# The mixing sub-layer of a two-layer trunk: conv's last projection traced before q's second half, the last tap written to SBUF, two attention steps traced between the value blocks

## The chip, the core and the metric

One Trainium2 chip, of which the kernel uses one core. The metric is the time in microseconds (us) of one execution on the device; where it was run several times, the median stands. A lower time is better.

## The reference, cut to what matters

The input is x of 512 tokens x 1024 features in float32. Two layers follow each other; each is half a SwiGLU network, a mixing sub-layer, and half a SwiGLU network again. The change touches only the mixing sub-layer:

```python
a, g, q, k, v = jnp.split(h @ w_in[l], splits, axis=-1)      # h = rms_norm(x, mix_norm[l]); 512 columns each
conv_out = conv_module(a, g, conv_w[l], conv_b[l], conv_norm[l])
q = rms_norm(q, q_norm[l]); k = rms_norm(k, k_norm[l])       # per head and map, 64 features each
diff_out = diff_attention(q, k, v, rel_bias, lam, lam_init, subln_norm[l])
x = x + jnp.concatenate([conv_out, diff_out], axis=-1) @ w_out[l]

def conv_module(a, g, conv_w, conv_b, conv_norm):
    u = a * jax.nn.sigmoid(g)
    y = causal_depthwise_conv(u, conv_w, width=31) + conv_b    # 512 channels
    return jax.nn.silu(rms_norm(y, conv_norm))                 # norm over the channels

# diff_attention, 4 heads, causal, swept over 4 blocks of 128 queries:
s = jnp.einsum("bhmqd,bhmkd->bhmqk", qi, k) * scale + bias     # m: two maps per head
p = jax.nn.softmax(s, axis=-1)
a = p[:, :, 0] - lam * p[:, :, 1]
o = jnp.einsum("bhqk,bhkd->bhqd", a, v)                        # then rms_norm per head, times (1 - lam_init)
```

`causal_depthwise_conv` stands for the call of `lax.conv_general_dilated` with 30 zeros of padding on the left.

## The kernel before, in words

**Precision.** Products of the projections and of the networks are made in three matmuls: weights and activations are each split into a rounded high part (`whi`, `acth`) and the rest (`wlo`, `actl`), and high x high, high x low and low x high are added up in PSUM. A weight chunk (`chunk`, L103) is loaded by a DMA on SP's queue into `wraw`, ACT copies it to `whi` (L100), and DVE or POOL subtracts to make `wlo` (L101). These three live in rings of 5, 4 and 4 buffers (`RING`, L90): a fifth chunk can only be converted when the chunk that used the slot first has been read by its last matmul. Scores, attention values and transposes are plain float32.

**PSUM.** The eight banks have tags (`BANKS`, L84): two each of `mm`, `sc` and `po`, one `tp`, one `y`. A projection takes a pair of banks, by turn `sc`, `po`, `mm` (`turn_tag`, L320; `pair_banks`, L323), in the order in which the code asks for them.

**Order.** The kernel is traced in a tile framework whose scheduler (`TileContext(..., schedule_with_timeline_sim=True)`, L931) sets the order of the instructions on each engine: it lists them with a modelled timeline, takes what is ready, and breaks ties by the order in which they were traced. A few instructions are pinned by `tc.keep_in_program_order`. So the order of the lines in `mixer` is a priority; it is not yet the order on the engines. Each engine then runs its own list in order and waits on semaphores.

**The mixing sub-layer** (`mixer`, L545) runs from about 355 to 540 us in the first layer and from 1246 to 1430 us in the second. Its steps, with the lines of the kernel before:

- `conv_in(c)` (L552), c = 0 to 3: two weight chunks, two projections of 24 matmuls each (gate and value of 128 conv channels), then the gate: DVE scales the gate by the rows' norm (L572), ACT takes tanh, DVE makes the value, POOL clears 30 columns, DVE writes `u`. c = 0 and 1 are multiplied together (`first_products`, L302).
- `project(which, pair)` (L589): k (which = 1) or q (which = 0), two token blocks (j) of 128 at a time. The four weight chunks of q or k are made at the first pair and kept for the second. 48 matmuls (L600 to L602) go into a pair of banks; ACT squares each block (L608), DVE sums the squares over 64 features (L609), POOL takes the power of -1/2 (`rsqrt`, L223), and DVE writes the normalised block `qn` (L615).
- `to_features(which, pair)` (L635): four transposes per block (L639) into the bank that the projection has left, then ACT copies them out to `kt` (L643) or, twice, to `qz`.
- `project_values(j)` (L621): 24 matmuls for one token block of v, and an ACT copy with the rows' norm.
- `conv_taps(c, n)` (L661): the 31 taps for conv channels c. The first n taps are made by ACT (a product, L671) and POOL (the sum), the others by DVE in a bank of PSUM (L676 or L679, then L684). `POOL_TAPS` = (31, 0, 0, 10): c = 0 is all ACT's and POOL's, c = 1 and 2 are all DVE's, and c = 3 is shared. The result goes to `ys[c]`: for c = 3 a sum of both parts on DVE (L688), for c = 1 and 2 an ACT copy out of PSUM (L690). `conv_square` (L653) squares it on ACT, POOL adds up `csum`.
- `conv_finish` (L693): the norm over channels (`rows_rstd` and `spread`, two passes of transposes), swish (L701 is its scale's product on DVE after ACT's tanh, L703 the low part).
- attention: 16 steps, block i = 3 to 0 and head h = 0 to 3. `attend(n)` (L782) traces the first part of step n and later parts of earlier steps, as a pipeline: `softmaxes` (L709) for step n: two score matmuls (L718), for both maps a DVE instruction that adds the bias and finds the row's minimum (L722) and an ACT exponential with a row sum (L726), then DVE's reciprocal (L729), a factor, and the difference of both maps; `keys_first` (L735) for step n-2: transposes of the map (L739) and an ACT copy (L741); `values` (L744) for step n-3: value matmuls (L748), and after the fourth head the norm per head, written by DVE as `ov` (L763); `block_out` (L771): four transposes and the split into `acth` and `actl`.
- the output projection (L819 to L834): in three rounds, first the conv half of the concatenated features for all tokens, then the attention half for tokens 256 to 511, then for tokens 0 to 255; 12 matmuls each go to a bank `sc` or `po` (`ps_out`), and DVE adds them to x.

**The order in which the body of `mixer` traces them** (L792 to L815): conv_in 0, 1, 2; both halves of k; q's first half with k's transposes around it; q's second half; q's first transposes; conv_in 3; q's last transposes; two attention steps, each with two value blocks behind it; the taps of c = 0 to 3; the attention steps from the third on; conv_finish; the output projection.

The only hand-written order is this one; the body of `mixer`, `conv_taps` and the functions that they call follow, with the lines of the profile.

Of the kernel before, what the change touches and what calls it, by code (L numbers as in the profile page):

```python
# [14 lines left out]
AF = mybir.ActivationFunctionType  # L15
ALU = mybir.AluOpType
# [4 lines left out]
SEQ = 512  # L21
DM = 1024
KT = DM // P
NT = SEQ // P
# [4 lines left out]
CT = CC // P  # L29
TAPS = 31  # L30
PAD = TAPS - 1
# [36 lines left out]
def trunk(ctx: ExitStack, tc: tile.TileContext, xt, par, lamv, relb, onehot,  # L68
          gu1, dn1, wag, wqkv, wout, gu2, dn2, out):
    nc = tc.nc  # L70
    V, S, G, T = nc.vector, nc.scalar, nc.gpsimd, nc.tensor
# [31 lines left out]
    def chunk(src, eng=None):  # L103
        raw, hi, lo = ring("wraw"), ring("whi"), ring("wlo")
        nc.sync.dma_start(raw, src)
        parts_of(raw, hi, lo, eng)
        return hi, lo
# [75 lines left out]
    pars = []  # L183
# [361 lines left out]
    def mixer(l, pr, after):  # L545
        with tc.tile_pool(name="mix", bufs=1) as mp, tc.tile_pool(name="mt", bufs=2) as mt:
            us = [None] * CT
# [4 lines left out]
            def conv_in(c):  # L552

                w = [chunk(wag[l, c, i], V if c < 3 else G) for i in range(2)]
                held.append((c, w, pair_banks(next(turn))))
                if c == 0:
                    return
                if c == 1:
                    row["c"], v, row["b"] = first_products(
                        pr, [h[1] for h in held], [h[2] for h in held], early=True  # L560
                    )

                    row["eps"] = small.tile([P, NT], F32, tag="rowe", name="rowe")
                    V.tensor_scalar(row["eps"], v, HD * EPS, None, op0=ALU.mult)

                    S.activation(small.tile([P, NT], F32, tag="rowx", name="rowx"), row["eps"], AF.Exp)
                else:
                    for i in range(2):
                        products(pr, w, held[-1][2][i], i)
                for n, _, ps in held:  # L570
                    gl = mt.tile([P, SEQ], F32, tag="gl", name="gl", bufs=1)
                    V.tensor_tensor(gl, ps[1], row["b"], op=ALU.mult)  # L572
                    S.activation(gl, gl, AF.Tanh, scale=0.5)
                    al = ps[0]
                    V.scalar_tensor_tensor(al, gl, 1.0, al, op0=ALU.add, op1=ALU.mult)
                    u = mp.tile([P, PAD + SEQ], F32, tag="u", name="u", bufs=4)
                    G.memset(u[:, :PAD], 0.0)
                    V.tensor_tensor(u[:, PAD:], al, row["b"], op=ALU.mult)
                    us[n] = u
                held.clear()  # L580
# [8 lines left out]
            def project(which, pair):  # L589
                if pair == 0:  # L590
                    wts[which] = [chunk(wqkv[l, which, kc], G) for kc in range(KT // 2)]
                w = wts[which]
                js = (2 * pair, 2 * pair + 1)
                ps = pair_banks(next(turn))
                for k in range(KT):
                    wh, wl = wpart(w[k // 2], k % 2, 512)
                    xh, xl = pr[k]
                    for n, j in enumerate(js):
                        t = slice(j * P, (j + 1) * P)
                        T.matmul(ps[n], xh[:, t], wh, start=k == 0, stop=False)  # L600
                        T.matmul(ps[n], xh[:, t], wl, start=False, stop=False)  # L601
                        T.matmul(ps[n], xl[:, t], wh, start=False, stop=k == KT - 1)  # L602

                ep = row["eps"][:, js[0] : js[1] + 1].unsqueeze(2).broadcast_to([P, 2, 8])
                ss = bank("tp", "ps_ss")[:, :16].rearrange("p (j g) -> p j g", j=2)
                for n, j in enumerate(js):
                    sq = tmp.tile([P, SEQ], F32, tag="sq", name="sq")
                    S.activation(sq, ps[n], AF.Square)  # L608
                    V.tensor_reduce(ss[:, n, :], sq.rearrange("p (g d) -> p g d", d=HD), axis=AX.X, op=ALU.add)  # L609
                v = small.tile([P, 2, 8], F32, tag="qkv", name="qkv", bufs=2)  # L610
                V.tensor_tensor(v, ss, ep, op=ALU.add)
                rq = rsqrt(v.rearrange("p j g -> p (j g)"), 16).rearrange("p (j g) -> p j g", j=2)
                for n, j in enumerate(js):
                    qn = mt.tile([P, SEQ], F32, tag="e0", name="qn", bufs=4)
                    V.tensor_tensor(  # L615
                        qn.rearrange("p (g d) -> p g d", d=HD), ps[n].rearrange("p (g d) -> p g d", d=HD),
                        rq[:, n, :].unsqueeze(2).broadcast_to([P, 8, HD]), op=ALU.mult,
                    )
                    qns[which, j] = qn, ps[n]
# [15 lines left out]
            def to_features(which, pair):  # L635
                for j in (2 * pair, 2 * pair + 1):
                    qn, pt = qns[which, j]
                    for h in range(HEADS):
                        T.transpose(pt[:, h * P : (h + 1) * P], qn[:, h * P : (h + 1) * P], ident)  # L639
                    pt = pt.rearrange("p (h t) -> p h t", h=HEADS)  # L640
                    t = slice(j * P, (j + 1) * P)
                    if which == 1:
                        S.activation(kt[:, :, t], pt, AF.Copy)  # L643
                    else:
                        for m in range(2):
                            S.activation(qz[:, m, :, t], pt, AF.Copy, scale=gq[l][:, m : m + 1])
# [3 lines left out]
            ys = [None] * CT  # L650
# [10 lines left out]
            def conv_taps(c, n):  # L661

                wc = _AT["conv_w"] + c * TAPS
                yp = None
                if n:
                    yp = mp.tile([P, SEQ], F32, tag="yp%d" % (n < TAPS), name="yp")
                    G.tensor_scalar(yp, us[c][:, 0:SEQ], pars[l][:, wc : wc + 1], col(l, "conv_b", c),
                                    op0=ALU.mult, op1=ALU.add)
                    for t in range(1, n):
                        p = mt.tile([P, SEQ], F32, tag="prod", name="prod")  # L670
                        S.activation(p, us[c][:, t : t + SEQ], AF.Copy, scale=pars[l][:, wc + t : wc + t + 1])  # L671
                        G.tensor_tensor(yp, yp, p, op=ALU.add)
                if n == TAPS:
                    ys[c] = yp
                    conv_square(c, yp)
                    return  # L676
                y = bank("y", "ps_y")
                if not n:
                    V.tensor_scalar(y, us[c][:, 0:SEQ], pars[l][:, wc : wc + 1], col(l, "conv_b", c),  # L679
                                    op0=ALU.mult, op1=ALU.add)  # L680
                else:
                    V.tensor_scalar(y, us[c][:, n : n + SEQ], pars[l][:, wc + n : wc + n + 1], None, op0=ALU.mult)
                for t in range(n + 1 if n else 1, TAPS):
                    V.scalar_tensor_tensor(y, us[c][:, t : t + SEQ], pars[l][:, wc + t : wc + t + 1], y,  # L684
                                           op0=ALU.mult, op1=ALU.add)
                ys[c] = us[c][:, PAD:]
                if n:
                    V.tensor_tensor(ys[c], y, yp, op=ALU.add)  # L688
                else:
                    S.activation(ys[c], y, AF.Copy)  # L690
                conv_square(c, ys[c])

            def conv_finish():  # L693
# [12 lines left out]
            steps = [(i, h) for i in reversed(range(NT)) for h in range(HEADS)]  # L706
# [75 lines left out]
            def attend(n):  # L782
                if n < len(steps):
                    softmaxes(*steps[n])
                if 2 <= n < len(steps) + 2:
                    keys_first(*steps[n - 2])
                if 3 <= n < len(steps) + 3:
                    values(*steps[n - 3])
                if n >= 5 and steps[n - 5][1] == HEADS - 1:
                    block_out(steps[n - 5][0])  # L790
# [5 lines left out]
            to_features(1, 0)  # L796
            project(0, 0)
            to_features(1, 1)
            project(0, 1)
            to_features(0, 0)  # L800
            conv_in(CT - 1)
            to_features(0, 1)
            bias = mp.tile([P, HEADS, SEQ], F32, tag="bias", name="bias")
            nc.sync.dma_start(bias, skew[0])
            row["bias"] = bias

            for n in range(2):
                attend(n)
                project_values(NT - 1 - 2 * n)
                project_values(NT - 2 - 2 * n)  # L810
            for c in range(CT):
                conv_taps(c, POOL_TAPS[c])
            for n in range(2, len(steps) + 5):
                attend(n)
            conv_finish()  # L815

# [119 lines left out]
```

## Time and profile before

| what | before |
|---|---|
| median of 3 runs | 1794.83 us (1794.76 to 1796.19) |
| the profiled execution | 1795.22 us, with a span of 1793.4 us |
| granted TensorE clock | 1.0 |
| matmuls on PE | 10861 |
| HBM read, mean rate | 227.26 MB, 129 GB/s |
| DMA packets' time on the two large queues, share of 16 engines | 33.2% and 12.5% |

PE is the TensorE matmul stream and PEld its weight loads; DVE, ACT, POOL and SP are the vector, scalar, general and sync engines. A row of a timeline gives the start in us from the span's begin, the duration, the engine, the line, the operation, what it writes and reads, the shape and type, "x8" for eight in a row, and in square brackets how long the engine had waited and for whom. The rows of the first mixing sub-layer by stage, as busy us of each engine:

```profile
411.00:446.00 35.00, 35.00 (x168) 29.20 (x168) 31.35 (x47) 19.28 (x29) 34.32 (x19) 1.00 0.40 120
446.00:460.00 14.00, 14.00 (x63) 10.93 (x62) 10.94 (x17) 9.27 (x15) 13.15 (x10) 1.00 0.26 76
512.00:540.00 28.00, 28.00 (x171) 24.99 (x170) 10.50 (x19) 5.97 (x8) 10.74 (x6) 1.00 0.23 75
```

Each row is a stretch, its length, and the busy us (and instructions) of PE, PEld, DVE, ACT and POOL, then the granted clock, the DMA engines' busy share and the GB/s moved. A matmul's record lasts longer than its turn, because matmuls are pipelined; a stretch with a full PE column can therefore still hide short waits, and these are found by comparing the starts of neighbouring matmuls.

### The profile page before, as it was taken

How to read it: one execution, taken by the hardware profiler on the slowest of the kernel's cores; microseconds unless marked ns; L12 is line 12 of the kernel's file. 1: busy time of each engine (PE TensorE's matmuls, PEld its weight loads, DVE VectorE, ACT ScalarE, POOL GpSimd, SP SyncE). 2: the span in 40 equal slices, each digit the busy share in tenths (PEclk: the TensorE clock that was granted, in tenths of full speed). 3: DMA queues.
4: the chain of work that ended last, by engine and by line, in shares of the span. 5: the costliest groups of instructions: out<-in, count | busy, mean ns of one | idle time of the engine just before them, and what ended most of it. 6: DMA issues, size and time to landing. Idle time of an engine off the chain costs nothing.

```text
span 1793.4 us, 28370 instructions
## 1 busy us (share of the span) xinstructions
PE 1783.9 (99%) x10861; PEld 1590.7 (89%) x10861; DVE 1199.0 (67%) x1849; ACT 896.4 (50%) x1483; POOL 646.6 (36%) x453
## 2 busy tenths in 40 slices
PE   9999999999999999999999999999999999999999
PEld 7899899888788899899888998998887888998997
DVE  6966477568867867467566764765788587674762
ACT  6455265445744456256433543654558354552651
POOL 2243243269843133142102312412798331322420
PEclk9999999999999999999999999999999999999999
DMA  7376466323212366466334654663231133664751
GB/s 246 103 182 180 112 162 191 116 96 94 71 48 83 94 165 189 106 171 190 104 95 98 168 170 120 175 182 117 71 116 50 48 106 92 169 175 108 182 152 59
DMA packets 111721, 231.24 MB, mean 129 GB/s; under 512 B 12151, under 2 KB 33414, under 8 KB 111584
## 3 DMA queue, kind: packets, MB, share of 16 engines
q1 hardware_dynamic: 91488, 191.93, 33.2%
q0 software_dynamic: 19808, 37.33, 12.5%
q8 instruction: 85, 1.39, 0.3%
q14 instruction: 52, 0.43, 0.1%
q10 hardware_dynamic: 288, 0.16, 0.0%
HBM read 227.26 MB, written 3.42 MB: 129 GB/s over the span
## 4 chain that ended last, share of the span: by engine, by line
PE 95%; DVE 3%; issue 1%; DMA 0%; ACT 0%; SPq 0%; ACTq 0%; DVEq 0%
PE ps_pair L384 38%; PE ps_d L172 9%; PE ps_d L175 9%; PE ps_d L176 9%; PE ps_pair L176 5%; PE ps_pair L175 5%; PE ps_pair L172 5%; PE ps_pair L602 2%; PE ps_pair L601 2%; PE ps_pair L600 2%; PE ps_out L175 1%; PE ps_sc L718 1%; PE ps_out L176 1%; PE ps_out L172 1%; DVE actl L261 1%; PE ps_v L632 1%
## 5 line engine op out<-in xcount | busy, mean ns | idle before, releaser
L100 ACT ACTIVATE whi<-wraw 128x512 fp32r<-128x512 f32 (+2 forms) x600 | 466.4, 801 | 610.9 <-PE ps_pair L384 226.7
L101 DVE TENSOR_TENSOR wlo<-wraw,whi 128x512 fp32r<-128x512 f32 (+2 forms) x557 | 516.5, 950 | 225.3 <-ACT whi L100 220.6
L384 PE MATMUL ps_pair<-acth,wlo 128*128 128x256 f32 x1088 | 307.9, 283 | 0.0
L384 PE MATMUL ps_pair<-actl,whi 128*128 128x256 f32 x1088 | 307.9, 283 | 0.0
L384 PE MATMUL ps_pair<-acth,whi 128*128 128x256 f32 x1088 | 307.9, 283 | 0.0
L175 PE MATMUL ps_d<-hl,whi 128*128 128x512 f32 x704 | 274.0, 389 | 0.0
L176 PE MATMUL ps_d<-hh,wlo 128*128 128x512 f32 x704 | 272.9, 389 | 0.0
L172 PE MATMUL ps_d<-hh,whi 128*128 128x512 f32 x704 | 269.1, 389 | 0.0
L384 PE MATMUL ps_pair<-th,wlo 128*128 128x256 f32 x816 | 230.9, 283 | 0.0
L384 PE MATMUL ps_pair<-tl,whi 128*128 128x256 f32 x816 | 230.8, 283 | 0.0
L384 PE MATMUL ps_pair<-th,whi 128*128 128x256 f32 x816 | 230.8, 283 | 0.0
L150 POOL DMA_DIRECT2D wraw<-in_gu x68 | 81.9, 1204 | 408.3 <-DMA wraw<-in_gu 158.2
L155 POOL TENSOR_TENSOR wraw<-wraw 128x512 f32<-128x512 f32 x68 | 108.2, 1591 | 329.6 <-DMA wraw<-in_gu 242.8
L384 PEld LDWEIGHTS ps_pair<-acth,whi 128*128 128x128 f32 x1088 | 208.9, 192 | 0.3
L384 PEld LDWEIGHTS ps_pair<-actl,whi 128*128 128x128 f32 x1088 | 208.9, 192 | 0.3
L384 PEld LDWEIGHTS ps_pair<-acth,wlo 128*128 128x128 f32 x1088 | 208.9, 192 | 0.0
L484 DVE SCALAR_TENSOR_TENSOR x<-ps_d,x 128x512 f32<-128x512 f32 x96 | 64.8, 689 | 180.5 <-PE ps_d L176 180.1
L175 PE MATMUL ps_pair<-actl,whi 128*128 128x512 f32 x448 | 174.8, 391 | 0.3
L172 PE MATMUL ps_pair<-acth,whi 128*128 128x512 f32 x448 | 173.8, 392 | 1.3 <-ACT whi L100 1.3
L176 PE MATMUL ps_pair<-acth,wlo 128*128 128x512 f32 x448 | 174.3, 390 | 0.0
L384 PEld LDWEIGHTS ps_pair<-tl,whi 128*128 128x128 f32 x816 | 156.5, 192 | 0.7
L384 PEld LDWEIGHTS ps_pair<-th,whi 128*128 128x128 f32 x816 | 156.5, 192 | 0.6
(169 smaller groups left out, 3248.7 us busy)
## 6 DMA issues: line engine op xcount, KB each, us to landing
wraw<-in_gu SPq DMA_DIRECT2D x208, 256.0 KB, 4.0
wraw<-in_gu SPq DMA_DIRECT2D x104, 512.0 KB, 3.7
wraw<-in_gu POOLq DMA_DIRECT2D x68, 512.0 KB, 5.7
wraw<-in_wqkv SPq DMA_DIRECT2D x24, 512.0 KB, 3.7
wraw<-in_dn SPq DMA_DIRECT2D x84, 128.0 KB, 3.0
wraw<-in_dn SPq DMA_DIRECT2D x32, 256.0 KB, 3.2
wraw<-in_wag SPq DMA_DIRECT2D x16, 512.0 KB, 3.6
wraw<-in_wout SPq DMA_DIRECT2D x16, 512.0 KB, 3.6
```

The lines of the kernel that those rows point to most:

```text
L100: S.activation(hi, raw, AF.Copy)
L101: (eng or V).tensor_tensor(out=lo, in0=raw, in1=f32(hi), op=ALU.subtract)
L150: nc.gpsimd.dma_start(two.rearrange("p (b c) -> p b c", b=2), u[:, h[0]].unsqueeze(1).broadcast_to([P, 2, 512]), accum_op=ALU.add)
L155: G.tensor_tensor(more[:, h[0]], two[:, h[1]], whole[:, h[0]], op=ALU.add)
L172: first = T.matmul(ps, wh, xh, start=start, stop=False)
L175: T.matmul(ps, wh, xl, start=False, stop=False)
L176: T.matmul(ps, wl, xh, start=False, stop=stop)
L384: mm = T.matmul(ps, l, r, start=first and i == j == 0, stop=False, skip_group_check=True)
L484: V.scalar_tensor_tensor(x[:, m, :], ps, 0.5, x[:, m, :], op0=ALU.mult, op1=ALU.add)
L600: T.matmul(ps[n], xh[:, t], wh, start=k == 0, stop=False)
L601: T.matmul(ps[n], xh[:, t], wl, start=False, stop=False)
L602: T.matmul(ps[n], xl[:, t], wh, start=False, stop=k == KT - 1)
```

## The change

Three things are changed, all in the mixing sub-layer of both layers.

1. In the body of `mixer`, `conv_in(CT - 1)` (conv's last projection) and `to_features(0, 0)` (q's first transposes) are traced before `project(0, 1)` (q's second half) instead of after it. With that, the pairs of banks that the two projections get by turn are exchanged.
2. In `conv_taps`, the last tap of channels whose taps are all on DVE (c = 1 and 2) writes the result into `us[c][:, PAD:]` in SBUF, and the copy by ACT from PSUM to that place goes. All earlier taps accumulate in PSUM as before. For c = 0 and 3 nothing changes.
3. The value blocks and the first attention steps, before `attend 0, pv 3, pv 2, attend 1, pv 1, pv 0`, then the taps, then `attend 2` and on, are traced as `attend 0, pv 3, pv 2, attend 1, pv 1, attend 2, pv 0, attend 3`, then the taps, then `attend 4` and on (pv j is `project_values(j)`).

No matmul, transfer or other computation is added; two ACT copies per layer go.

```diff
--- before.py
+++ after.py
@@ -680,14 +680,13 @@
                                     op0=ALU.mult, op1=ALU.add)
                 else:
                     V.tensor_scalar(y, us[c][:, n : n + SEQ], pars[l][:, wc + n : wc + n + 1], None, op0=ALU.mult)
+
+                ys[c] = us[c][:, PAD:]
                 for t in range(n + 1 if n else 1, TAPS):
-                    V.scalar_tensor_tensor(y, us[c][:, t : t + SEQ], pars[l][:, wc + t : wc + t + 1], y,
-                                           op0=ALU.mult, op1=ALU.add)
-                ys[c] = us[c][:, PAD:]
+                    V.scalar_tensor_tensor(ys[c] if t == PAD and not n else y, us[c][:, t : t + SEQ],
+                                           pars[l][:, wc + t : wc + t + 1], y, op0=ALU.mult, op1=ALU.add)
                 if n:
                     V.tensor_tensor(ys[c], y, yp, op=ALU.add)
-                else:
-                    S.activation(ys[c], y, AF.Copy)
                 conv_square(c, ys[c])
 
             def conv_finish():
@@ -796,21 +795,25 @@
             to_features(1, 0)
             project(0, 0)
             to_features(1, 1)
+            conv_in(CT - 1)
+            to_features(0, 0)
             project(0, 1)
-            to_features(0, 0)
-            conv_in(CT - 1)
             to_features(0, 1)
             bias = mp.tile([P, HEADS, SEQ], F32, tag="bias", name="bias")
             nc.sync.dma_start(bias, skew[0])
             row["bias"] = bias
 
-            for n in range(2):
-                attend(n)
-                project_values(NT - 1 - 2 * n)
-                project_values(NT - 2 - 2 * n)
+            attend(0)
+            project_values(3)
+            project_values(2)
+            attend(1)
+            project_values(1)
+            attend(2)
+            project_values(0)
+            attend(3)
             for c in range(CT):
                 conv_taps(c, POOL_TAPS[c])
-            for n in range(2, len(steps) + 5):
+            for n in range(4, len(steps) + 5):
                 attend(n)
             conv_finish()
```

## The prediction

> **What bounds the kernel now.** I read the page first: the span and the busy time by engine.
>
> ```profile
> span 1793.4 us, 28370 instructions
> PE 1783.9 (99%) x10861; PEld 1590.7 (89%) x10861; DVE 1199.0 (67%) x1849; ACT 896.4 (50%) x1483; POOL 646.6 (36%) x453
> ```
>
> PE is the bound nearly everywhere, and the change takes no matmul away and adds none. So the time can move only through the moments in which PE stands still. Where are they? The busy time by windows over the first mixer, and over the attention of the second, says:
>
> ```profile
> 460.00:480.00 20.00, 20.00 (x88) 14.47 (x86) 16.45 (x42) 18.97 (x38) 19.30 (x13) 1.00 0.23 62
> 480.00:512.00 32.00, 30.39 (x183) 23.76 (x182) 29.56 (x104) 25.61 (x75) 15.90 (x16) 1.00 0.09 29
> 1371.00:1403.00 32.00, 30.38 (x181) 23.78 (x180) 30.04 (x104) 25.42 (x74) 15.20 (x16) 1.00 0.07 23
> ```
>
> The columns are window, its length, busy us of PE, PEld, DVE, ACT and POOL, then the granted clock. Value blocks and first scores (460 to 480) leave PE no gap. The tail of attention (480 to 512) does, equally in both layers. There DVE is busy 29.56 of 32 us: it is the local bound. The gaps are larger than 1.6 us, because a matmul's record (0.39 us) lasts longer than its turn: PE starts the next one 0.227 us later. The first and the last of some 28 late starts in PE's timeline, with one between:
>
> ```profile
> 488.01 0.55 PE L739 MATMUL ps_at<-ident,e 128*128 128x128 f32 x3 [0.43 <-ACT at L741]
> ...
> 504.37 0.48 PE L172 MATMUL ps_out<-acth,whi 128*128 128x512 f32 x1
> ...
> 510.03 0.71 PE L172 MATMUL ps_out<-acth,whi 128*128 128x512 f32 x2
> 510.73 0.50 PE L175 MATMUL ps_out<-actl,whi 128*128 128x512 f32 x1
> ```
>
> Two matmuls take 2 x 0.227 us, so 510.73 stands 0.25 us late. Counted so, start to start, PE loses about 5.7 us in the tail of each mixer, 4.3 of them before 504.37 and 1.4 after. These 2 x 5.7 us are all that the change can win. What it can lose has no such limit.
>
> **The change part by part.** The scheduler decides the order, so I take the built orders of both programs. DMA issues on SP are the same in both. POOL's order is the same up to the second group of k (j = 2, 3): weights' low parts, products, the reciprocal root.
>
> *Conv's last projection ahead of q's second half.* It does not go ahead. Its weight chunks need slots of the four-deep whi ring, and q's four chunks hold all of them until q's second half has read them. In the built order all of q's matmuls still stand before those of conv_in(3). What changes is around it: the two now swap their pair of PSUM banks, so q's second half writes into the banks of k's second half. It must wait until k's transposes (L639) are done and ACT has copied them out (L643). And those transposes now come after 46 projection matmuls instead of 72. Their operands do not come sooner:
>
> ```profile
> 411.28 1.03 PE L639 MATMUL ps_pair<-ident,qn 128*128 128x128 f32 x8
> ...
> 428.49 1.04 PE L639 MATMUL ps_pair<-ident,qn 128*128 128x128 f32 x8
> ```
> ```profile
> 419.60 2.94 POOL L223 TENSOR_TENSOR rs_y<-qkv,mhalf 128x16 f32<-128x16 f32 x1
> ```
> ```profile
> 410.97 0.69 DVE L609 TENSOR_REDUCE ps_ss<-sq 128x8 f32<-128x512 f32 x1 [0.20 <-ACT sq L608]
> ...
> 414.67 0.81 DVE L679 TENSOR_SCALAR ps_y<-u,par 128x512 f32<-128x512 f32 x1 [1.54 <-ACT u L690]
> 415.52 7.09 DVE L684 SCALAR_TENSOR_TENSOR ps_y<-u,par,ps_y 128x512 f32<-128x512 f32 x9
> 422.57 1.29 DVE L615 TENSOR_TENSOR qn<-ps_pair,rs_y 128x512 f32<-128x512 f32 x2
> ```
> ```profile
> 410.34 1.28 ACT L608 ACTIVATE sq<-ps_pair 128x512 f32<-128x512 f32 x2 [0.98 <-PE ps_pair L602]
> ...
> 413.56 0.60 ACT L643 ACTIVATE kt<-ps_pair 128x512 f32<-128x512 f32 x1
> 414.03 0.60 ACT L690 ACTIVATE u<-ps_y 128x512 f32<-128x512 f32 x1
> ```
>
> The transposes start at 428.49 now; 26 x 0.227 = 5.9 us sooner is 422.6. The root that qn needs ends on POOL at 422.54 in either order. So qn (L615) cannot be there before 423.2, a stall of 0.65 us at the least. And DVE has ten taps ahead of it, a reduction (L609) of q's squares and one more tap. Those squares are ready when q's first half ends on PE (421.7 + 0.39) and ACT has squared it (0.60): 422.75. Reduction, tap and qn take 0.61 + 0.65 + 0.68, so the first qn is there at 424.7, and the transposes run from 424.75 instead of 422.6. Then four transposes (0.44), the copy (0.60) and its signals pass before q's second half may start: about 425.9, against 423.5 without waits. **An early stall of 2.5 us in each mixer**, where PE has no gap today. PE's in-order queue holds all later projections behind it, so ACT's and POOL's conversions, conv_in(3) and the first scores come 2.5 us later. The DVE then runs dry at conv_in(3)'s gate:
>
> ```profile
> 446.38 0.69 DVE L572 TENSOR_TENSOR gl<-ps_pair,rb 128x512 f32<-128x512 f32 x1 [0.30 <-PE ps_pair L176]
> ```
> ```profile
> 458.79 0.69 DVE L722 CUSTOM_DVE_ANT_0 e<-ps_sc,bias 128x512 f32<-128x512 f32 x1 [1.02 <-PE ps_sc L718]
> ...
> 473.36 0.69 DVE L722 CUSTOM_DVE_ANT_0 e<-ps_sc,bias 128x512 f32<-128x512 f32 x1 [2.52 <-PE ps_sc L718]
> ```
>
> The gate moves from 446.4 to about 449.2, the first score from 458.8 to 461.2. I bound the early stall by 0.65 us (DVE free as soon as POOL is) and 3 us, and take 2.5.
>
> *Last tap into SBUF.* Two ACT copies (L690) of 0.60 us go in each mixer, and the wait of 1.54 us for the first, above. The last taps write SBUF; the trace shows taps with PSUM as output (0.75 us, the x9 row), and the nearest row with SBUF as output is the final sum (L688):
>
> ```profile
> 486.23 0.69 DVE L688 TENSOR_TENSOR u<-ps_y,yp 128x512 f32<-128x512 f32 x1
> ```
>
> The one wait that is added, ACT's square of the last tap's output, is behind the same tap as the copy was. Between 0 and -0.07 us each, I take 0. What is won on DVE is lost again ahead of L572: after the early stall DVE waits there for PE, so these 1.5 us buy nothing.
>
> *Third and fourth steps ahead of value blocks.* In the built order the third score stands behind 24 value matmuls instead of 48, which should fill the 2.52 us hole above. These rows of ACT matter:
>
> ```profile
> 473.09 1.05 ACT L100 ACTIVATE whi<-wraw 128x1024 fp32r<-128x1024 f32 x1
> 474.03 0.71 ACT L671 ACTIVATE prod<-u,par 128x512 f32<-128x512 f32 x1
> ```
>
> Behind that score, the new order makes the reciprocal of the third step wait on ACT. Its second exponential stands behind the conversions of W_out's chunks (L100, 1.05 us each, released only as the last value block reads its weights, here from 471.7 on) and products (L671, 0.71). Three conversions, two products, an exponential and a copy of about 0.6 each, less 0.1 at each change, make 6 us and put it at 477.0 to 477.7, and DVE idles for about 2.5 us at that reciprocal. The hole moves rather than goes. If ACT is clear in time, up to 2.5 us of DVE time are won: I keep both ends and take the hole as moved, because POOL, which paces ACT's products, is as full as before (19.30 of 20 us).
>
> *The sum in the tail.* The last long wait of PE is for the second block's normalised output (ov, L763). The rows of DVE's timeline from the third step's reciprocal to it, with the first and the last of the three waits between:
>
> ```profile
> 476.99 0.16 DVE L729 RECIPROCAL r<-sums 128x1 f32<-128x1 f32 x1
> ...
> 481.18 0.57 DVE L722 CUSTOM_DVE_ANT_0 ps_sc<-ps_sc,bias 128x384 f32<-128x384 f32 x1 [0.95 <-PE ps_sc L718]
> ...
> 485.12 0.16 DVE L729 RECIPROCAL r<-sums 128x1 f32<-128x1 f32 x1 [0.43 <-ACT ps_sc L726]
> ...
> 503.06 0.69 DVE L763 TENSOR_TENSOR ov<-ps_o,rs_y 128x512 f32<-128x512 f32 x1
> ```
>
> From 476.99 to the end of that ov (503.75) DVE takes 26.8 us, and waits for 2.0 of them. In the new order the same stretch holds one L701, one L703 and two wide L722 more, and two narrow L722 and a reciprocal less: +2.0 us, so 26.8 us without a wait. It starts at 477.75. With no wait ov ends at 504.5, with waits as now at 506.5; between such ends I take the middle, 505.5, since the scores come as late to DVE as DVE comes to them. Four transposes later, at 506.0, PE reaches the output matmuls that it reaches at 504.37 now: +1.63. At this point 4 output matmuls (0.91) and 2 pairs of value matmuls (0.43) are still to do that are done now: +1.34. On the other side these output matmuls then stand 14 in a row, conv's outputs being ready, and cover attention's last steps; of the 1.4 us of later waits I let 0.64 go. Together 1.63 + 1.34 - 0.64 = **+2.3 us per mixer**: the tail hands on nearly all of the 2.5 us. For two mixers +4.7. On the profiled execution (1795.22 us: its span and 1.8 us around it) that is 1799.9; it stands 0.4 over the median, so on the median 1794.83 + 4.7 = **1799.5 us**. Waits of 0 or 2.0 us give +1.3 or +3.3 per mixer: 1797.5 to 1801.5.
>
> A stall has a second price, if the clock falls:
>
> ```profile
> L196 PE MATMUL ps_idle<-ones_r x9: 453/628/796, 1.0 to 4.6; 128*128 128x512 f32 x9
> ```
> ```profile
> 10.14 0.50 PE L172 MATMUL ps_pair<-acth,whi 128*128 128x512 f32 x1 [0.91 <-ACT whi L100]
> ```
>
> The first matmuls of the program come 0.45 us apart (8 steps from 1.0 to 4.6) instead of 0.227. Eight such steps after the stall cost 1.8 us per mixer. The granted clock reads 1.00 in all windows above, over waits of half a us, and PE's longest later wait is the 0.91 us of the second row. The Trainium skill, in "TensorE: Matmul & The Clock Gate", section "What's actually happening", says that PE falls back to half its clock after an idle window of about 3.4 us. By that rule a stall of 2.5 us would keep the clock and one of 3.4 would not; no run here shows a gap of that length.
>
> **The rivals.** My forecast is slower by more than can be missed: a measurement of this kernel tells about 0.2%, 3.6 us. Chance 0.45, with its own range of 1797.5 to 1801.5.
> *The tail takes the stall up.* DVE goes through the new stretch without a wait, because the scores were issued well before it comes to them, and conv's early outputs fill PE's other waits. Then +1.3 us per mixer at most, and nothing where ACT's exponential also comes before the conversions (ov 1.5 us sooner): 1794.8 to 1797.5, say 1796.2. This is not slower by what can be told. It decides from the point where DVE's waits in the stretch fall under 0.5 us (+1.8 per mixer). For it: the third score is traced earlier. Against it: 29.56 busy us of 32. Chance 0.27.
> *Faster.* The 2.52 us hole is filled and conv's sum leaves the tail's way (L688, at 486.23 now, may run at about 480.5). Of 5.7 us of tail waits 1.2 would remain: 2.5 - 4.5 = -2 per mixer, 1790.8. For it: both long waits of DVE in these rows, 1.54 and 2.52 us, lose the instruction that ends them. Against it: DVE's load is the same. Chance 0.20.
> *Slower by the clock.* 1799.5 + 2 x 1.8 = 1803.1, if the early gap is long enough. Against it: the clock stays at 1.00 through every wait above, the longest of 0.91 us. Chance 0.08.
> That the change does nothing of what it says is half true (the projection stays behind q), and alone would give 1794.8, at the edge of the second case.
>
> **How the numbers follow.** Of the forecast case's 0.45 I give 0.38 to slower by over 0.2% (1798.4 and more) and 0.07 to less; the clock gives slower 0.08, the second case 0.03 slower and 0.24 same, the third 0.17 faster and 0.03 same. That makes faster 0.17, same 0.34, slower 0.49. To leave out no more than 2 in 10 (the clock's 0.08 and half of the third case), the range goes from that case's 1790.8 over the second case and the forecast's own range, with 0.5 us for a measurement's spread: 1790.8 to 1802.0.
>
> **What would show it.** Right: PE waits about 2 us ahead of the second group of L639 in each mixer, released by DVE's qn, and again ahead of the next L600, released by ACT's kt. DVE waits 2 to 6 us ahead of the fourth L572, and about 2.5 us at the third step's reciprocal, released by ACT. In the tail PE is late by about as much as the 5.7 us now. Wrong: no wait at those transposes, since qn came sooner than POOL's queue lets me think; a granted clock under 1.00 after them; a tail whose waits shrink by 2 us or more.

## The result and the profile after

The changed kernel takes **1802.14 us** (median of 6 runs, 1801.00 to 1802.91), the kernel before 1794.80 us in the 6 runs beside it: 7.3 us more, a ratio of 1.0042 with a 95% interval of 1.0032 to 1.0051. The forecast was 1799.5 us, with a range to 1802.0, so the median lies 0.14 us above the range. The profiled execution took 1802.91 us. Its page:

```profile
span 1801.1 us, 28362 instructions
PE 1784.8 (99%) x10861; PEld 1593.3 (88%) x10861; DVE 1198.0 (67%) x1849; ACT 893.7 (50%) x1479; POOL 638.4 (35%) x453
```

The work is the same and the span 7.7 us longer, so PE stands or runs slower somewhere. The busy time by windows of the changed kernel (window, length, busy us of PE, PEld, DVE, ACT and POOL, granted clock, DMA share, GB/s):

```profile
425.00:430.00 5.00, 4.91 (x17) 3.80 (x17) 4.86 (x9) 2.23 (x4) 4.75 (x3) 0.66 0.00 0
480.00:512.00 32.00, 28.41 (x181) 23.42 (x180) 31.09 (x104) 26.09 (x75) 15.57 (x14) 1.00 0.18 50
...
1320.00:1325.00 5.00, 5.00 (x18) 4.17 (x18) 4.86 (x9) 2.22 (x4) 4.73 (x3) 0.69 0.00 0
500.00:505.00 5.00, 2.75 (x18) 2.32 (x19) 5.00 (x20) 4.90 (x15) 1.08 (x3) 1.00 0.01 3
505.00:510.00 5.00, 4.21 (x26) 3.36 (x26) 5.00 (x20) 3.80 (x13) 0.38 (x1) 1.00 0.00 0
```

The new thing is the granted clock: 0.66 and 0.69, once in each mixer, where the kernel before has 1.00. It stands in PE's timeline at k's second transposes:

```profile
421.80 0.39 PE L602 MATMUL ps_pair<-whi,actl 128*128 128x512 f32 x1
424.23 1.25 PE L639 MATMUL ps_pair<-ident,qn 128*128 128x128 f32 x8 [2.04 <-DVE qn L615]
425.57 0.80 PE L600 MATMUL ps_pair<-whi,acth 128*128 128x512 f32 x1
426.16 0.63 PE L601 MATMUL ps_pair<-wlo,acth 128*128 128x512 f32 x1
426.59 0.63 PE L602 MATMUL ps_pair<-whi,actl 128*128 128x512 f32 x1
...
428.30 0.63 PE L600 MATMUL ps_pair<-whi,acth 128*128 128x512 f32 x1
428.72 0.46 PE L601 MATMUL ps_pair<-wlo,acth 128*128 128x512 f32 x1
```

Read the starts. From 421.80 the next instruction should come at 422.03; it comes at 424.23, released by DVE's qn. With the small gaps among the transposes PE loses 2.75 us here. Then the matmuls start 0.43 us apart (426.16, 426.59) instead of 0.227, up to 428.72: another 1.64 us. Windows set to this stretch show where it begins and ends:

```profile
422.03:425.44 3.41, 1.37 (x9) 0.84 (x8) 3.21 (x6) 2.01 (x5) 3.25 (x3) 1.00 0.07 24
425.44:428.85 3.41, 3.32 (x9) 2.63 (x9) 3.30 (x6) 1.79 (x4) 3.15 (x2) 0.50 0.00 0
428.85:432.26 3.41, 3.41 (x17) 2.78 (x16) 3.34 (x6) 1.21 (x2) 3.25 (x4) 1.00 0.00 0
```

The granted clock is a half for 3.41 us, behind a window of the same length in which PE's records cover 1.37 us; the second mixer has the same from 1319.73 to 1323.15. Counted start to start, as in the prediction:

| PE's loss per mixer, us | before | after, first mixer | after, second mixer |
|---|---|---|---|
| wait at k's second transposes | 0 | 2.75 | 2.75 |
| half turns behind it | 0 | 1.64 | 1.29 |
| from the first score to the end of the mixer | 5.8 | 6.2 | 5.4 |

That makes 8.4 us for both mixers, with the tails level in sum; the profiled execution is 7.7 us longer, since its first mixer began 0.6 us sooner. Not every execution has both half stretches. One lowers the mean clock by about 0.001; the three executions at a mean of 0.998 took 1802.65 to 1802.91 us, the one at 1.000 took 1801.00. So in the time the two stretches cost about 1.9 us, less than the 2.9 counted at the place. DVE's rows of the changed kernel:

```profile
422.23 0.69 DVE L609 TENSOR_REDUCE ps_ss<-sq 128x8 f32<-128x512 f32 x1 [1.25 <-ACT sq L608]
422.83 0.75 DVE L686 SCALAR_TENSOR_TENSOR ps_y<-u,par,ps_y 128x512 f32<-128x512 f32 x1
423.49 1.28 DVE L615 TENSOR_TENSOR qn<-ps_pair,rs_y 128x512 f32<-128x512 f32 x2
...
450.56 0.69 DVE L572 TENSOR_TENSOR gl<-ps_pair,rb 128x512 f32<-128x512 f32 x1 [5.93 <-PE ps_pair L176]
...
462.75 0.69 DVE L721 CUSTOM_DVE_ANT_0 e<-ps_sc,bias 128x512 f32<-128x512 f32 x1 [1.00 <-PE ps_sc L717]
...
476.17 0.70 DVE L721 CUSTOM_DVE_ANT_0 ps_sc<-ps_sc,bias 128x512 f32<-128x512 f32 x1 [0.76 <-PE ps_sc L717]
...
479.10 0.16 DVE L728 RECIPROCAL r<-sums 128x1 f32<-128x1 f32 x1 [2.17 <-ACT ps_sc L725]
...
506.68 0.69 DVE L762 TENSOR_TENSOR ov<-ps_o,rs_y 128x512 f32<-128x512 f32 x1
```

A reduction that waits for ACT's square of q, one tap, and only then qn: that chain ends the wait of PE (the first qn ends at about 424.2). The gate of conv's last projection comes at 450.56 (446.38 before), the first score at 462.75 (458.79), and the hole of 2.5 us at the third step's score is now one of 0.76 at the score and one of 2.17 at the reciprocal, released by ACT.

### The profile page after: what moved, and what is told of

Its sections match the earlier page's. It is cut to its first block, busy times and chain, and to the rows that moved or that the text cites. A ratio compares the mean times of both kernels' runs of the same rounds, so it can differ in the third digit from the quotient of the medians.

```text
span 1801.1 us, 28362 instructions
## 1 busy us (share of the span) xinstructions
PE 1784.8 (99%) x10861; PEld 1593.3 (88%) x10861; DVE 1198.0 (67%) x1849; ACT 893.7 (50%) x1479; POOL 638.4 (35%) x453
## 4 chain that ended last, share of the span: by engine, by line
PE 95%; DVE 4%; issue 1%; DMA 1%; POOL 0%; ACT 0%; ACTq 0%; DVEq 0%; POOLq 0%
PE ps_pair L384 38%; PE ps_d L175 9%; PE ps_d L176 9%; PE ps_d L172 9%; PE ps_pair L176 5%; PE ps_pair L175 5%; PE ps_pair L172 5%; PE ps_pair L600 2%; PE ps_pair L601 2%; PE ps_pair L602 2%; PE ps_out L176 1%; PE ps_out L175 1%; PE ps_out L172 1%; PE ps_sc L717 1%; DVE actl L261 1%; PE ps_v L631 1%
## 5 line engine op out<-in xcount | busy, mean ns | idle before, releaser
L155 POOL TENSOR_TENSOR wraw<-wraw 128x512 f32<-128x512 f32 x68 | 101.4, 1491 | 324.8 <-DMA wraw<-in_gu 281.3
```

What stands on the lines that cost most here:

```text
L155: G.tensor_tensor(more[:, h[0]], two[:, h[1]], whole[:, h[0]], op=ALU.add)
```

## The experiments

Theory A: the loss is the early wait with the half clock behind it, and the tail hands both on. Theory B: the loss comes from the new order of value blocks and attention steps. "Early" and "tail" are PE's losses per mixer, start to start, up to the first score and from there on; ratios are to the kernel before on the same chip. Each edit also lets the scheduler find a new order, so a small difference cannot be put down to the edited lines alone.

### Banks given back

```diff
-            turn = iter(range(12))
+            turn = iter((0, 1, 2, 3, 4, 5, 7, 6))
```

> The changed kernel, with the turns of the two projections exchanged, so that q's second half gets the sc banks again and conv's last projection the po banks. The built order then has k's second transposes behind 74 projection matmuls instead of 46. Theory A (the loss is PE's wait ahead of these transposes, because q's second half needs their banks, with the half clock after it, and the tail hands it on): no wait there, granted clock 1.00, and a time within 2 us of the kernel before, 1793 to 1797. Theory B (the loss comes from the new order of the value blocks and attention steps, and the tail would have taken an early wait up): the tail is as in the changed kernel, so 1799 to 1802.

Measured: 1797.79 us, ratio 1.0016 (1.0007 to 1.0026). Windows of this kernel:

```profile
410.00:440.00 30.00, 30.00 (x142) 25.03 (x141) 27.81 (x43) 15.58 (x23) 29.33 (x16) 1.00 0.39 115
...
1390.00:1395.00 5.00, 3.22 (x17) 2.75 (x18) 4.96 (x17) 3.68 (x14) 3.02 (x4) 0.85 0.00 0
1395.00:1400.00 5.00, 5.00 (x27) 4.33 (x26) 4.64 (x16) 4.65 (x13) 1.17 (x2) 0.81 0.00 0
```

PE is full from 410 to 440 and the early wait is gone; two exchanged numbers take away some 4 of the 7.3 us. It stays 3.4 us slower, more than theory A allowed and less than theory B: 0.9 us per mixer is lost later, at q's transposes, and the tail loses 6.1 and 6.8 us, the second with the clock at 0.85 and 0.81.

### Without part 1

The lines of part 1 in their old order, parts 2 and 3 kept.

> The changed kernel with the first part undone: q's second half is traced ahead of q's first transposes and conv's last projection again; the last tap in SBUF and the two attention steps between the value blocks stay. Theory A: no early wait, 1793 to 1797. Theory B: as slow as the changed kernel, 1799 to 1802.

Measured: 1795.83 us, ratio 1.0007 (0.9999 to 1.0016). Theory A holds and B falls. Early below 0.1, tail 6.4 us per mixer: parts 2 and 3 together cost some 0.6 us in each tail, no more.

### The wait filled

```diff
             project(0, 0)
+            for n in range(2):
+                ps = bank("sc", "ps_fill")
+            for n in range(9):
+                mm = T.matmul(ps, ones_r, ones_r.unsqueeze(1).broadcast_to([P, NT, P]), start=True, stop=True)
+                tc.keep_in_program_order(mm)
             to_features(1, 1)
```

> The changed kernel with nine more matmuls of ones (128x512, into a free bank; nothing reads the result) pinned between q's first half and k's second transposes: 9 x 0.227 = 2.04 us of work in the wait of 2.2 us. The built order is otherwise that of the changed kernel. Theory A with the half clock as a term of its own: the wait's 2.75 us stay, the 1.64 and 1.25 us of matmuls at half turn behind it go, so 2.9 us less than 1802.1 at the most: 1799 to 1800.5, granted clock 1.000. Theory C (the half clock costs nothing in the end, because the matmuls behind it would wait in the tail anyway): 1801.5 to 1802.5 with the clock at 1.000.

Measured: 1800.82 us (1800.32 to 1802.52), ratio 1.0038 (1.0025 to 1.0050). A window of this kernel:

```profile
425.00:430.00 5.00, 5.00 (x22) 4.14 (x23) 4.86 (x9) 1.84 (x4) 4.67 (x4) 1.00 0.00 0
```

The clock behind the transposes is 1.00 again. The early loss, fill included, falls from 4.4 and 4.0 to 2.9 us in both mixers, the tail loses 6.2 in both, and the profiled execution is 2.5 us shorter (1800.37 against 1802.91): the half clock is a term of its own. The medians differ by only 1.3 us, and 1800.82 lies between the cases of A and C: two of the five executions took 2 us longer than the others at a mean clock of 0.998. So the clock also falls elsewhere at times, as the last experiment shows in the tail. Against the kernel without part 1, 2.8 us more of early loss per mixer made 5.0 us in the time: the tail hands on nine tenths of it.

### Part 1 alone

> The kernel before with the first part alone: conv's last projection and q's first transposes traced ahead of q's second half. Built, k's second transposes stand behind 46 projection matmuls, as in the changed kernel; the taps and the attention steps are as before. Theory A: the early wait and the half clock are there, 1799 to 1803. Theory B: the loss isn't there, 1794 to 1796.

Measured: 1798.37 us (1797.09 to 1801.98), ratio 1.0023 (1.0013 to 1.0033). That lies between the two theories. The early wait is there, as theory A says, but it is shorter, and no half clock follows it. PE's and DVE's rows:

```profile
426.30 1.26 PE L639 MATMUL ps_pair<-ident,qn 128*128 128x128 f32 x8 [1.33 <-DVE qn L615]
427.64 0.50 PE L600 MATMUL ps_pair<-whi,acth 128*128 128x512 f32 x1
427.98 0.39 PE L601 MATMUL ps_pair<-wlo,acth 128*128 128x512 f32 x1
```
```profile
424.96 0.69 DVE L609 TENSOR_REDUCE ps_ss<-sq 128x8 f32<-128x512 f32 x1 [0.15 <-ACT sq L608]
425.57 1.28 DVE L615 TENSOR_TENSOR qn<-ps_pair,rs_y 128x512 f32<-128x512 f32 x2
```

Here no tap stands between the reduction and qn, PE loses 2.1 us instead of 2.75, and the turns behind it are 0.23 us at once (427.98 and on). The clock does fall in the tail of the second mixer:

```profile
1394.84:1398.26 3.42, 1.66 (x11) 1.23 (x11) 3.36 (x10) 3.05 (x10) 1.71 (x2) 1.00 0.00 0
1398.26:1401.67 3.41, 3.41 (x10) 2.88 (x11) 3.41 (x12) 2.94 (x9) 0.00 (x0) 0.50 0.00 0
```

That tail loses 7.0 us; the first mixer's, at full clock, loses 4.9. The three executions at a mean clock of 1.000 took 1797.09 to 1797.36 us, some 2.8 us over the kernel before, for 2 x 2.1 us of early loss: here the tail takes up a part. (This profiled execution, at 1801.98 us, also lost 2.7 us near 130 us, outside the mixers.)

### Part 2 alone and part 3 alone

> The kernel before with the second part alone: the last tap of conv's channels c = 1 and 2 writes SBUF, two ACT copies per layer less. The runs so far give 1795.8 for the second and third part together (1794.4 for the kernel before beside them), 0.65 us more waits in the tail of each mixer. Theory D (the third part makes these waits, the second is worth nothing): 1794 to 1794.8. Theory E (the second part makes them, because the taps end at another moment): 1795.5 to 1796.2.

> The kernel before with the third part alone: the third and fourth attention steps traced between the value blocks. Theory D (this part makes the 0.65 us of additional waits in the tail of each mixer, since DVE's hole of 2.5 us at the third step's score comes back at its reciprocal): 1795.3 to 1796.2. Theory E: 1794 to 1794.8. If the hole were filled and DVE came into the tail earlier: 1791 to 1793.

Part 2 alone: **1792.69 us, ratio 0.9989 (0.9980 to 0.9998)**, the fastest of all; against the kernel before the gain is just clear of the noise. Part 3 alone: 1794.97, ratio 1.0002 (0.9993 to 1.0011), no difference that can be told, and between the cases of D and E. For part 2 both theories fail; neither had a gain. The tail of part 2 alone loses 5.0 us per mixer against 5.8 before, that of part 3 alone 6.1. The tail's window with part 2 alone:

```profile
480.00:512.00 32.00, 30.89 (x185) 24.53 (x184) 29.71 (x105) 25.68 (x74) 15.64 (x16) 1.00 0.06 18
```

PE's records cover half a us more of it than before, DVE's as much as before.

### Conv's last projection really ahead of q

```diff
             to_features(1, 0)
+            conv_in(CT - 1)
             project(0, 0)
             to_features(1, 1)
             project(0, 1)
             to_features(0, 0)
-            conv_in(CT - 1)
             to_features(0, 1)
```

> The kernel before with the last tap in SBUF, and conv's last projection traced ahead of both halves of q, so that its matmuls really stand ahead of q's in the built order. It has no second half of q that waits for banks: no early wait, clock 1.00. Theory F (conv's last taps come 11 us earlier to DVE and fill its idle time, and the tail is bound by DVE): tail waits under 4 us per mixer, 1790 to 1793. Theory G (q's square root then has nothing to hide behind but value blocks, the first scores stand behind all 96 value matmuls, 11 us later, and DVE has to catch up in the tail): waits of PE at the scores, 1797 to 1806.

Measured: 1797.68 us, ratio 1.0016 (1.0007 to 1.0025): theory G. The first score in DVE's timeline:

```profile
468.81 0.69 DVE L721 CUSTOM_DVE_ANT_0 e<-ps_sc,bias 128x512 f32<-128x512 f32 x1 [5.78 <-PE ps_sc L717]
```

PE starts the first score at 467.75, with part 2 alone at 456.50. DVE gets conv's last taps earlier, but then waits 5.78 us in one piece; the tail loses 7.4 us per mixer. It is 5.0 us slower than part 2 alone, on which it is built.

### Conv's low parts off DVE

```diff
-                    V.scalar_tensor_tensor(cl[:, c, :], z, hg, f32(ch[:, c, :]), op0=ALU.mult, op1=ALU.subtract)
+                    S.activation(z, z, AF.Copy, scale=hg)
+                    G.tensor_tensor(cl[:, c, :], z, f32(ch[:, c, :]), op=ALU.subtract)
```

> The kernel before with the last tap in SBUF, and conv's low parts taken off DVE: four multiply-subtracts of 0.74 us per mixer become four ACT scalings and four POOL subtractions. If DVE's load bounds the tail, 3 us less on DVE should take 1 to 2.5 us of waits per mixer: 1790 to 1793. If the tail is bound by the chain of one step after another (score, minimum, exponential, difference) and not by the load, or POOL's subtractions come too late for the output matmuls: 1794 to 1798.

Measured: 1795.17 us, ratio 1.0002 (0.9994 to 1.0011), 2.5 us more than part 2 alone, on which it is built. The tail's window:

```profile
480.00:512.00 32.00, 29.67 (x182) 23.79 (x181) 27.06 (x99) 28.08 (x79) 20.33 (x20) 1.00 0.07 24
```

DVE has 2.65 us less to do in these 32 us and PE still stands longer. So DVE's load alone does not bound the tail. What does is not shown: the edit also gives ACT 2.4 us and POOL 4.7 us more to do there, and the sequence of the steps, ACT's load and late subtractions on POOL are not told apart.

### Parts 1 and 2, parts 1 and 3

> The changed kernel with the third part undone (parts 1 and 2 together). Alone they gave +4.0 and -1.9 us. If the two add up: 1796.6. The prediction's claim that what the last tap in SBUF wins on DVE is lost again behind the early wait: 1798.4, as part 1 alone. If the early wait also costs the half clock here as in the changed kernel: 1800 to 1802. The early wait itself is there in all three cases.

> The changed kernel with the second part undone (parts 1 and 3 together). Alone they gave +4.0 and +0.4 us. If the two add up: 1798.9. If the early wait and the third part's order of the value blocks hurt each other in the tail: 1800.5 to 1803. The early wait is there in both cases; with the ACT copies kept it starts later and should be about 1.5 us long, as in part 1 alone, too short to bring half the clock.

Measured: parts 1 and 2 together, outside all three cases, 1808.16 us (1803.27 to 1810.35), ratio 1.0068 (1.0054 to 1.0082); parts 1 and 3 together 1799.55, ratio 1.0030 (1.0019 to 1.0042). Parts 1 and 3 add up about as expected (1798.9), and behind their early wait the clock stays at 1.00; it falls for one stretch in the second mixer's tail, from 1390.98. Parts 1 and 2 do not add up: two parts that give +4.0 and -1.9 alone give +14.1. Windows of their profiled execution (1810.35 us):

```profile
425.00:430.00 5.00, 5.00 (x19) 4.00 (x18) 4.86 (x8) 2.30 (x4) 4.73 (x3) 0.68 0.00 0
505.00:510.00 5.00, 3.17 (x15) 2.64 (x14) 4.04 (x15) 3.13 (x11) 0.00 (x0) 0.67 0.00 0
510.00:515.00 5.00, 5.00 (x17) 3.93 (x16) 2.22 (x10) 1.11 (x5) 0.00 (x0) 0.65 0.00 0
```

The clock falls twice in each mixer, behind the early wait and again in the tail, where PE loses 9.5 us per mixer. The early wait is 2.21 us ahead of the transposes wherever part 2 goes with part 1, and 1.49 without it (start to start). What differs is the one tap (L686) between reduction and qn: without the wait for ACT's copy DVE is further on with its taps (it waits 1.25 us for that reduction instead of 0.15), and one more of them is built in there.

| parts | 1 | 2 | 3 | 1+2 | 1+3 | 2+3 | 1+2+3 |
|---|---|---|---|---|---|---|---|
| us against the kernel before beside it | +4.0 | -1.9 | +0.4 | +14.1 | +5.5 | +1.5 | +7.3 |

### Part 2 with a copy put back

```diff
                 if n:
                     V.tensor_tensor(ys[c], y, yp, op=ALU.add)
+                else:
+                    S.activation(mt.tile([P, SEQ], F32, tag="csq", name="csq", bufs=1), ys[c], AF.Copy)
```

> Part 2 alone, with an ACT copy of the finished result into a scratch tile added for channels c = 1 and 2, so that ACT has the two copies per layer again (nobody reads them) but DVE no longer waits 1.54 us for one. Part 2 alone gave 1792.7. If it gains through DVE's wait: 1792.5 to 1793.2. If it gains through ACT's time, or through the order of the tail that the scheduler happens to find with it: 1794 to 1796.

Measured: 1795.96 us, ratio 1.0008 (0.9999 to 1.0017), 3.3 us more than part 2 alone. So the gain of part 2 is not DVE's wait of 1.54 us alone, which is gone here too. Whether it is ACT's time or the order of the tail that the scheduler finds (it differs between these two kernels) stays open.

### The wait half filled

The loop of the filled wait with 4 instead of 9.

> The changed kernel with four instead of nine more matmuls of ones in front of k's second transposes: 0.9 us of the wait of 2.2 us filled, 1.3 us left; the built order is otherwise that of the changed kernel. If half the clock needs a stretch of some 3.4 us without wide matmuls, as between 422.0 and 425.6 in the changed kernel: no half turn behind the wait, and the time of the kernel with nine, 1800 to 1801. If a single wait of about 1 us is enough: half turns behind it as in the changed kernel, 1801.5 to 1803.

Measured: 1801.83 us (1800.54 to 1802.49), ratio 1.0038 (1.0024 to 1.0051). Windows and PE's rows of the profiled execution (1802.49 us):

```profile
425.00:430.00 5.00, 5.00 (x22) 4.13 (x23) 4.86 (x9) 1.84 (x4) 4.70 (x4) 1.00 0.00 0
...
500.00:505.00 5.00, 2.94 (x17) 2.39 (x16) 5.00 (x18) 3.70 (x11) 1.20 (x2) 0.89 0.01 3
505.00:510.00 5.00, 5.00 (x23) 4.36 (x22) 4.72 (x18) 3.65 (x13) 0.00 (x0) 0.77 0.00 0
```
```profile
501.29 0.49 PE L717 MATMUL ps_sc<-kt,qz 128*128 128x128 f32 x2 [1.16 <-DVE mn L721]
...
502.59 0.49 PE L717 MATMUL ps_sc<-kt,qz 128*128 128x128 f32 x2 [0.36 <-DVE e L731]
...
503.83 1.19 PE L747 MATMUL ps_o<-vv,at 128*128 128x128 f32 x4 [0.53 <-ACT at L740]
...
506.38 0.78 PE L172 MATMUL ps_out<-acth,whi 128*128 128x512 f32 x1
506.95 0.57 PE L175 MATMUL ps_out<-actl,whi 128*128 128x512 f32 x1
```

Half a fill is enough behind the early wait: no half turn there, as the first case said. But the time went the way of the second, since the clock now falls in the tail, behind a run of short waits (1.16, 0.36, 0.53 us and one before them). The changed kernel has much the same waits in its tail (2.75 busy us from 500 to 505 in the windows above) and kept 1.00 there in its profiled execution. The windows of 3.41 us tell the two apart, the first row of the changed kernel, the others of this one:

```profile
500.53:503.95 3.42, 2.06 (x14) 1.82 (x15) 3.42 (x13) 3.42 (x12) 0.00 (x0) 1.00 0.00 0
...
500.48:503.89 3.41, 1.71 (x11) 1.28 (x11) 3.41 (x12) 2.62 (x8) 1.20 (x2) 1.00 0.02 5
503.89:507.30 3.41, 3.41 (x14) 3.29 (x15) 3.13 (x12) 2.90 (x11) 0.00 (x0) 0.50 0.00 0
```

Half stretches start on a fixed grid: in the changed kernel the two starts, 425.44 and 1319.73, are 262 x 3.413 us apart, and within each profile every distance between starts is such a multiple. In the 14 profiles, without their first and last 10 us, a window of this grid at full clock was followed by half the clock in all 11 cases in which PE's records covered at most 1.88 us of it, and in none with 1.89 us or more. So it matters how a run of waits falls onto the grid.

## Why the prediction failed, point by point

- **What bounds it, and the bank.** Right: PE is full, and the exchange of the banks makes q's second half wait for k's transposes (the banks given back, and the kernel without part 1).
- **Early wait, 2.5 us.** 2.75 measured, with the chain as worked out (squares, reduction, tap, qn, then ACT's copy to kt). The tap in it, which the prediction read from the order, belongs to part 2.
- **The clock: the step that failed.** The prediction set the half clock aside as a rival of chance 0.08 and left it out of sum and range, because the clock "stays at 1.00 through every wait above, the longest of 0.91 us". Waits below 1 us say nothing of one of 2 us, and what counted was not the gap alone: from the end of the last wide matmul's record (422.19) to the next wide one (425.57) 3.4 us pass with only eight transposes, and PE's records cover 1.37 of the 3.41 us ahead of the half clock. The execution without a half stretch took 1801.00 us, inside the range; those with two took 1802.65 and more, outside it. The price it gave, 1.8 us per mixer, was near what is lost at the place, 1.64 and 1.29, and nearly twice what shows in the time, about 0.95. That rival's 1803.1 us is the nearest of all cases to 1802.14, in part by luck: its clock costs too much and its early wait too little. The Trainium skill, in "TensorE: Matmul & The Clock Gate", section "What's actually happening", speaks of an idle window of about 3.4 us that runs freely. The half turns here last 3.41 us and start on a fixed grid, which agrees, but the window ahead of them was not idle. The prediction compared the stall alone with 3.4 us.
- **What the tail hands on.** Forecast 2.3 of 2.5 us per mixer; the tails lose 6.2 and 5.4 us against 5.8, so all of it in sum. With 2 x 2.75 instead of 2 x 2.3 the prediction's sum is 1800.3, against 1801.00 in the execution at full clock, and with the half clock in one mixer 1801.6 to 1802.0, in both 1803.3. The 0.7 us between 1800.3 and 1801.00 have no cause that the runs show.
- **DVE's late gates.** Forecast 449.2 for the fourth L572 and 461.2 for the first score; 450.56 and 462.75 measured. The differences, 1.4 and 1.6 us, are about the half turns' 1.64. The second block's ov ended at 507.37 instead of 505.5, likely for the same reason.
- **The hole at the third score moves rather than goes.** Right: 0.76 us at the score, 2.17 at the reciprocal, released by ACT.
- **Part 2 taken as nothing.** Wrong. Alone it gives -1.9 us; with part 1 it costs, by the tap ahead of qn and the half clock that follows.
- **DVE as the tail's local bound.** Not borne out: 2.65 us less DVE work did not shorten the tail. What bounds it stays open.

What stays open: by what part 2 alone gains 1.9 us, what bounds the tail, and which kinds of PE's work count towards the clock.

## What to carry to other kernels

With a scheduler, moving a block in the traced order may leave its work where it is and change only what rotates with it, here the pair of PSUM banks: look in the built order for who waits for the buffers that change hands. Price a wait of PE of about 2 us in a full stretch at the wait and up to 1.6 us of half clock behind it, and judge by PE's share of a window of 3.4 us, not by its longest gap. Measure the parts of a change alone and in pairs before adding them up: part 2 by itself gives the fastest version here (1792.7 us), and together with part 1 the slowest (1808.2 us).

## What the runs showed of the hardware

The granted clock fell to a half for 3.41 us not only behind a standing wait of 2.0 us (PE's records covering 1.37 of the 3.41 us ahead, in the changed kernel), but also behind a run of waits of 0.4 to 1.2 us between small matmuls (1.71 of 3.41 us, in the half-filled kernel). The half stretches start on a grid of 3.41 us, and in these profiles a window covered to at most 1.88 us brought one and a window covered to 1.89 us or more did not. With parts 1 and 2 together the clock stayed at a half for two windows in a row in each tail, with records at half clock covering 2.89 us of the first. The changed kernel's own executions spread from 1801.0 us at a mean clock of 1.000 to 1802.9 at 0.998; the kernel before stayed at 1.000 in every run beside the experiments.
